# The first modulation of a diffusion layer: where three blocks sum their shift tiles, and which engine makes one affine

## The chip, the core and the metric

The kernel runs on one core of one Trainium2 chip. The time is the device time of one execution in microseconds; the time of a kernel is the median of its runs. One further execution is recorded by the profiler; its instructions, engines and waits are what "the profile" and "the trace" mean below. The engines are TensorE (PE in the profile; PEld are its weight loads), VectorE (DVE), ScalarE (ACT), GpSimd (POOL) and SyncE (SP), whose queue issues most of the DMA transfers.

## The reference

One layer of a diffusion backbone over 256 context tokens and 256 latent tokens of width 2048: a half-step SwiGLU feed-forward, token mixing, a second half-step feed-forward and a final norm. Ahead of each part stands an RMSNorm with a shift and a scale that come from a condition vector. What the change touches is the first of them, for both sequences:

```
def rms_norm(x, g):
    xf = x.astype(jnp.float32)
    y = xf * lax.rsqrt(jnp.mean(xf * xf, axis=-1, keepdims=True) + RMS_EPS)
    return (y * g.astype(jnp.float32)).astype(x.dtype)

def adaln(x, g, mod, i):
    return rms_norm(x, g) * (1 + mod[:, i + 1, None, :]) + mod[:, i, None, :]

def half_step_ffn(x, mod, i, g, w_up, w_down):
    h = adaln(x, g, mod, i)
    a, b = jnp.split(h @ w_up, 2, axis=-1)
    return x + 0.5 * mod[:, i + 2, None, :] * ((jax.nn.silu(a) * b) @ w_down)
...
        mod_l = (silu_c @ w_mod[l] + b_mod[l]).reshape(B, N_MOD, D_MODEL)
        mod_c = (silu_cc @ w_mod[l] + b_mod[l]).reshape(1, N_MOD, D_MODEL)
        xl = half_step_ffn(xl, mod_l, 0, g_norm[l, 0], w_ffn1_up[l], w_ffn1_down[l])
        xc = half_step_ffn(xc, mod_c, 0, g_norm[l, 0], w_ffn1_up[l], w_ffn1_down[l])
```

Everything is float32. The kernel keeps that precision by splitting an operand into a rounded part and the rest (`hi` and `lo`, `hhi` and `hlo`) and adding three products.

## The kernel before

**Tiles and blocks.** The width of 2048 is cut into 16 contraction tiles of 128 columns. In the beginning (lines 460 to 690) shift and scale of the first norm are computed tile by tile, together with the first products of the up projection: `BLOCKS` holds tiles 0 and 1 as blocks of one, then seven blocks of two (2 and 3, 4 and 5, up to 14 and 15). The code names a block by its bounds `k0`, `k1`.

**Shift and scale of a block.** Each is a product of a vector of 2048 (SiLU of the condition, one for each sequence) with 128 columns of `w_mod`. There are two ways.

On TensorE (`mod_sums`, line 563): a unit of weights (`mraw`, 128 x 2048, 1 MB) is multiplied with `cP`, the two condition vectors as 32 columns. The four strips of the array work on different contraction tiles, so a PSUM buffer holds four partial sums. ScalarE copies it to `row`; `mod_turned` (line 587) transposes the row on TensorE into another PSUM buffer, and VectorE reduces that to the column of `SH` (shift) or `SC` (scale) and adds the bias (`biased`).

On VectorE (lines 658 to 662): the unit lies transposed, and one SCALAR_TENSOR_TENSOR of 2048 columns for each sequence multiplies it with `cB`, the condition spread over all partitions, and sums along the row into `SH`.

In a block of two, VectorE sums the shift of the first tile and TensorE that of the second tile (`mod_sums(0, k1 - 1, k1)`, one unit of 16 multiplications, two records each) and the scales of both tiles (`mod_sums(1, k0, k1)`, two units of 8 wider ones). That is four units for a block. `mod_unit` loads them in the order of use into a ring of four `mraw` buffers (`bufs=4`, line 559), on SP's queue, which takes its loads in order.

**What follows in a block.** After the sums come `mod_turned`, `scale_of` (the scale times the gain of the norm), and `to_hT` (line 368), once for each sequence: TensorE transposes x into a PSUM buffer, and `affine_split` makes hhi, h and hlo from it. ScalarE makes both tiles of hhi and the first of h, VectorE the second of h (line 387) and hlo = h - hhi.

**Filler.** `products` (line 406) is a generator: the matmuls of a block with the weights of the first six halves of the up projection, in six steps of six matmuls for a block of two. The products of the block before (`prods`) are issued between the sums of this one, the last two steps after `to_hT` (`drain(prods)`). The weights of this block's products (`following`) are loaded between the units of scale and split on ScalarE (hi) and VectorE (lo) ahead of `mod_turned`.

**Order.** In this stage VectorE, TensorE and SP's loads keep the order of the program (`Pinned`, `keep_in_program_order`), ScalarE's order is left to the scheduler from the block of tile 2 on. `tbank` gives the PSUM buffers of this stage: a ring of two, for the sums, for the turned rows and for the transposed x alike. Each waits until the one two places before it was read.

Recorded operations have line 87 in the profile where a helper issues them, so tiles and not lines tell them apart.

Of the kernel before, what the change touches and what calls it, by code (L numbers as in the profile page):

```python
# [12 lines left out]
FP8 = mybir.dt.float8e5  # L13
AF = mybir.ActivationFunctionType
# [5 lines left out]
P = 128  # L20
# [20 lines left out]
PACE += (86, 102), (92, 109), (98, 118), (100, 130), (103, 144), (106, 152), (109, 163), (112, 170), (128, 181)  # L41

BLOCKS2 = tuple((k, k + 4) for k in range(0, 16, 4))

BLOCKS = ((0, 1), (1, 2)) + tuple((k, k + 2) for k in range(2, 16, 2))
FB = 4
# [12 lines left out]
def tile_layer(ctx: ExitStack, tc: tile.TileContext, I: dict, out: bass.AP):  # L59
# [319 lines left out]
    def affine_split(src, n, pairs, hh, hl):  # L379

        h = scratch[-1].tile([P, 2, 256], F32, tag="h", name="h", bufs=2)
        cols = [(SC[:, n, s, k : k + 1], SH[:, n, s, k : k + 1]) for k, s in pairs]
        if n != 1:
            for kk, (sc, sh) in enumerate(cols):
                scalar[0].activation(hh[:, kk, :], src[:, kk, :], AF.Identity, scale=sc, bias=sh)
        scalar[0].activation(h[:, 0, :], src[:, 0, :], AF.Identity, scale=cols[0][0], bias=cols[0][1])
        vector[0].tensor_scalar(h[:, 1, :], src[:, 1, :], *cols[1], op0=ALU.mult, op1=ALU.add)
        if n == 1:
            scalar[0].activation(hh, h, AF.Copy)
        vector[0].tensor_tensor(hl, h, hh.bitcast(F32), op=ALU.subtract)  # L390
# [70 lines left out]
    with pool(name="st", bufs=1) as st:  # L461
# [94 lines left out]
        def mod_unit():  # L556
            if ready:
                return ready.pop(0)
            raw = st.tile([P, 2048], F32, tag="mraw", name="mraw", bufs=4)
            tc.keep_in_program_order(nc.sync.dma_start(raw, I["w_m0"][next(unit)]))  # L560
            return raw

        def mod_sums(i, k0, k1, last=iter(())):

            n = (k1 - k0) * P
            nk = 2048 // n
            b = tbank()[:, :n]
            for g in range(KT // nk):
                if g == KT // nk - 1:
                    steps(last)  # L570
                raw = mod_unit()
                for j in range(nk):
                    k = nk * g + j
                    q = 32 * (j % 4)
                    tensor[0].matmul(
                        b[q : q + 32, :], cP[:, k, :], raw[:, j * n : (j + 1) * n], start=k < 4, stop=k >= KT - 4, tile_position=(0, q), skip_group_check=True
                    )
                yield
            row = st.tile([P, 256], F32, tag="row", name="row", bufs=3)[:, :n]
            scalar[0].activation(row, b, AF.Copy)  # L580
            turns.append((i, k0, k1, row))

        def biased(i, k0, k1):
            dst = (SH, SC)[i][:, 0, :, k0:k1]
            vector[0].tensor_tensor(dst, dst, bmT[:, i, k0:k1].unsqueeze(1).to_broadcast([P, 2, k1 - k0]), op=ALU.add)
# [61 lines left out]
        for k0, k1 in BLOCKS[1:]:  # L647
            kk = slice(k0, k1)
            following = products(1, pre, k0, k1, hhi, hlo, middle=True)
            if k1 - k0 == 2:  # L650
                raw = mod_unit()
            for i in range(2):
                for _ in mod_sums(i, k0 if i else k1 - 1, k1, following if i else iter(())):
                    steps(prods, 3 - (k1 - k0))
                if rest:
                    others(2, True)
                if not i and k1 - k0 == 2:
                    for s in (CTX, LAT):
                        vector[0].scalar_tensor_tensor(
                            junk.bitcast(FP8), raw, 1.0, cB[:, s, :], op0=ALU.mult, op1=ALU.mult, accum_out=SH[:, 0, s, k0 : k0 + 1], saturate=False  # L660
                        )
                    biased(0, k0, k0 + 1)

            if k0 != 2:
                steps(following)
            mod_turned()
            if k0 != 2:
                steps(prods)
            for s in (CTX, LAT):
                scale_of(0, s, kk)  # L670
            if k0 == 2:
                steps(following)
                steps(prods)
            if k1 - k0 == 1:
                tb = tbank()
                for s in (CTX, LAT):
                    for t in range(2):
                        x_turned(k0, s, t, tb)
                x_scaled(k0, tb)
            else:  # L680
                for s in (CTX, LAT):
                    drain(to_hT([xs0[s, 0], xs0[s, 1]], 0, s, hhi, hlo, 256 * s, range(k0, k1)))
            drain(prods)
            prods = following
            if k0 == 2:
                scalar[0] = nc.scalar
            if k1 == KT:
                nc.sync.dma_start(ccd.rearrange("s (k p) -> (s k) p", p=P), cc)
# [1659 lines left out]
def _laid_out(a):  # L2348
    asc = np.ascontiguousarray
    part = lambda v: v.reshape(-1, P).T  # L2350
    m = {
        "x": asc(a["x"][0]),
        "ctx": asc(a["ctx"][0]),
        "cc": asc(np.concatenate([a["c_ctx"].reshape(KT, P), a["c"].reshape(KT, P)])),
        "b_mod": asc(a["b_mod"][0].reshape(9, D)),
        "gate_b": asc(a["gate_b"][0]),
        "m_gain": asc(a["m_gain"][0]),
        "q_gain": asc(a["q_gain"][0]),
        "k_gain": asc(a["k_gain"][0]),
        "g_final": asc(a["g_final"]),  # L2360
        "rope": _rope_tables(),
    }
    cw = a["conv_w"][0].T.reshape(16, P, 5).transpose(1, 0, 2).reshape(P, 80)
    m["vecs"] = asc(np.concatenate([part(a["b_mod"][0]), part(a["g_norm"][0]), cw, part(a["conv_b"][0])], 1))

    wm = a["w_mod"][0].reshape(D, 9, D)

    def units(i, a_, b):
        n = (b - a_) * P
        k = 2048 // n  # L2370
        return wm[:, i, a_ * P : b * P].reshape(KT // k, k, P, n).transpose(0, 2, 1, 3).reshape(KT // k, P, 2048)

    def block(k0, k1):

        still = [wm[:, 0, k0 * P : (k0 + 1) * P].T[None]] if k1 - k0 == 2 else []
        return still + [units(0, k1 - 1, k1), units(1, k0, k1)]

    m["w_m0"] = asc(np.concatenate([u for b in BLOCKS for u in block(*b)]))
    m["w_mt"] = asc(wm[:, 2:].reshape(D, 7, KT, P).transpose(1, 2, 3, 0))
    for n in "12":  # L2380
        up, dn = a[f"w_ffn{n}_up"][0], a[f"w_ffn{n}_down"][0]
        nf = dn.shape[0] // P
        up = up.reshape(KT, P, 2, nf, P)

        rest = up[:, :, :, FB:].reshape(4, 4, P, 2, nf // FB - 1, CB)
        m[f"w_up{n}b"] = asc(rest.transpose(4, 3, 0, 2, 1, 5).reshape(nf // FB - 1, 2, 4, P, 2048))
        first = up[:, :, :, :FB].transpose(3, 2, 1, 0, 4).reshape(-1, 2, P, 2048)
        m[f"w_up{n}"] = asc(first[NPRE:])
        pre = first[:NPRE].reshape(2 * NPRE, P, KT, P)
        loads = []  # L2390
        for k0, k1 in BLOCKS if n == "1" else BLOCKS2:
            most = min(2 * NPRE, 2048 // ((k1 - k0) * P) // 2 * 2)
            loads += [pre[u : u + most, :, k0:k1].transpose(1, 0, 2, 3).ravel() for u in range(0, 2 * NPRE, most)]
        m[f"w_pre{n}"] = asc(np.concatenate(loads))
        m[f"w_dn{n}"] = asc(dn.reshape(NF // FB, FB, P, NCB, CB).transpose(0, 3, 2, 1, 4).reshape(NF // FB, NCB, P, 2048))
    w = a["w_in"][0]

    def tokens_still(cols):
        n = cols.shape[1]
        return asc(cols.reshape(4, 4, P, n).transpose(0, 2, 1, 3).reshape(4, P, 4 * n))  # L2400

    def tokens_move(c0):
        return asc(w[:, c0 : c0 + 1024].reshape(KT, P, NH, P).transpose(2, 1, 0, 3).reshape(NH, P, 2048))

    m["w_a"] = tokens_still(np.concatenate([w[:, GT0:], w[:, MV0 : MV0 + 384]], 1))
    m["w_b"] = tokens_still(w[:, MV0 + 384 : MV0 + 768])
    m["w_c"] = asc(w[:, MV0 + 768 : MV0 + 1024].reshape(2, 8, P, 256).transpose(0, 2, 1, 3).reshape(2, P, 2048))
    m["w_mk"], m["w_mq"] = tokens_move(MK0), tokens_move(MQ0)
    m["w_kv"] = tokens_still(w[:, AK0 : AK0 + 512])
    for c in range(2):  # L2410
        m[f"w_q{c}"] = tokens_still(w[:, AQ0 + 512 * c : AQ0 + 512 * (c + 1)])
        m[f"w_o{c}"] = tokens_still(w[:, MO0 + 512 * c : MO0 + 512 * (c + 1)])
    m["w_out"] = asc(a["w_out"][0].reshape(4, 4, P, NCB, CB).transpose(3, 0, 2, 1, 4).reshape(NCB, 4, P, 2048))
    return m
# [15 lines left out]
```

## Time and profile before

| | |
|---|---|
| time, median of 3 runs | 2605.07 us (2602.81 to 2609.3) |
| profiled execution, its time | 2604.58 us |
| its span in the trace | 2602.7 us |
| mean granted clock of TensorE | 0.996 |
| the beginning up to the last block's products | 0 to 126.5 us |

In the rows of the timeline the columns are start and length in us, engine, line, operation, the tiles written and read (`tr` and `mm` are PSUM buffers, `raw` the weights of products, `junkv` what the sums write beside their result), shapes, count, and in brackets the idle time before it with what ended it. A row with a count merges neighbours that run on. The chain of waits is the work that ended last, followed back; in its rows stand start, length, engine and tile. A matmul's length contains its latency, so the pace is read from starts.

### The profile page before, as it was taken

The page shows a single profiled execution, that of the slowest core. Times are in us where ns is not written, and L with a number is a line of the kernel's source. Part 1 is how long each engine was busy: PE and PEld are TensorE (multiplying, and loading weights), DVE is VectorE, ACT ScalarE, POOL GpSimd, SP SyncE. Part 2 cuts the span into 40 slices and gives each one's busy share as a digit, 9 for nine tenths or more (in the row PEclk, how much of TensorE's full clock was granted, in tenths as well). Part 3 has the DMA queues.
Part 4 walks back from the last instruction along what each step waited for, and adds up shares of the span by engine and source line. Part 5 has one row for each costly group of instructions (what it writes and reads, how often), then busy time and mean ns, then how long its engine had stood idle before and what let it go on. Part 6 is the DMA issues. An engine that isn't in the chain of part 4 may idle for free.

```text
span 2602.7 us, 33781 instructions
## 1 busy us (share of the span) xinstructions
PE 2575.7 (99%) x12670; PEld 2144.7 (82%) x12670; DVE 2170.6 (83%) x2864; ACT 1417.7 (54%) x1810; POOL 220.7 (8%) x269
## 2 busy tenths in 40 slices
PE   8999999999999999999999999999999999999998
PEld 5788888888888888888889889888897888888887
DVE  7788888878888788888887889798889878887887
ACT  4454444544444565444454347456476676666664
POOL 0000000100000100000110000120000000000001
PEclk8999999999999999999999999999999999999999
DMA  9889999999999988889987887776768988999876
GB/s 392 350 217 265 276 277 271 262 273 285 261 287 265 278 247 240 218 215 228 225 253 266 296 312 247 242 273 213 267 239 240 269 269 260 272 273 279 256 231 176
DMA packets 127219, 681.01 MB, mean 262 GB/s; under 512 B 14152, under 2 KB 16712, under 8 KB 64976
## 3 DMA queue, kind: packets, MB, share of 16 engines
q1 hardware_dynamic: 98544, 493.25, 50.7%
q0 software_dynamic: 28512, 185.61, 36.4%
q8 instruction: 99, 1.62, 0.2%
q14 instruction: 64, 0.52, 0.1%
HBM read 660.91 MB, written 17.89 MB: 261 GB/s over the span
## 4 chain that ended last, share of the span: by engine, by line
PE 85%; DVE 7%; DMA 5%; issue 2%; ACT 1%; POOL 0%; ACTq 0%; POOLq 0%; SPq 0%; DVEq 0%
PE mm L151 21%; PE mm L150 21%; PE mm L149 21%; DVE lo L128 2%; PE mm L87 2%; PE Y L149 2%; PE Y L151 2%; PE Y L150 2%; PE X L151 2%; PE X L150 2%; PE X L149 2%; PE tr L150 1%; PE tr L149 1%; PE tr L151 1%; PE tr L87 1%
## 5 line engine op out<-in xcount | busy, mean ns | idle before, releaser
L127 ACT ACTIVATE hi<-raw 128x1024 fp32r<-128x1024 f32 (+2 forms) x500 | 517.8, 1041 | 421.1 <-PE mm L151 264.1
L128 DVE TENSOR_TENSOR lo<-raw,hi 128x1024 fp32r<-128x1024 f32 (+2 forms) x488 | 583.6, 1207 | 149.7 <-ACT hi L127 130.5
L127 ACT ACTIVATE hi<-chain 128x1024 fp32r<-128x1024 f32 x336 | 355.0, 1059 | 305.7 <-PE mm L151 188.0
L128 DVE TENSOR_TENSOR lo<-chain,hi 128x1024 fp32r<-128x1024 f32 x336 | 407.2, 1221 | 118.0 <-ACT hi L127 114.3
L149 PE MATMUL mm<-hi,hhi 128*128 128x512 f32 (+3 forms) x1024 | 393.6, 385 | 0.0
L151 PE MATMUL mm<-hi,hlo 128*128 128x512 f32 (+3 forms) x1024 | 386.7, 378 | 0.0
L150 PE MATMUL mm<-lo,hhi 128*128 128x512 f32 (+3 forms) x1024 | 386.7, 378 | 0.0
L207 DVE SCALAR_TENSOR_TENSOR junk<-sraw,cBh 128x1024 fp8e5<-128x1024 f32 x192 | 234.3, 1220 | 19.2 <-DMA sraw<-in_w_mt 16.7
L151 PEld LDWEIGHTS mm<-hi,hlo 128*128 128x128 f32 x1024 | 192.5, 188 | 33.9
L149 PEld LDWEIGHTS mm<-hi,hhi 128*128 128x128 f32 x1024 | 192.6, 188 | 31.0
L150 PEld LDWEIGHTS mm<-lo,hhi 128*128 128x128 f32 x1024 | 192.8, 188 | 30.7
L128 DVE TENSOR_TENSOR lo<-ra,hi 128x1024 fp32r<-128x1024 f32 x96 | 117.0, 1223 | 39.7 <-ACT hi L127 35.8
L127 ACT ACTIVATE hi<-ra 128x1024 fp32r<-128x1024 f32 x96 | 101.9, 1061 | 65.1 <-PE mm L151 48.4
L149 PE MATMUL mm<-hi,hid2h 128*128 128x512 f32 x352 | 137.1, 390 | 0.0
L151 PE MATMUL mm<-hi,hid2l 128*128 128x512 f32 x352 | 137.0, 389 | 0.0
L150 PE MATMUL mm<-lo,hid2h 128*128 128x512 f32 x352 | 136.9, 389 | 0.0
L207 DVE SCALAR_TENSOR_TENSOR sr<-sr,cBl 128x1024 f32<-128x1024 f32 x84 | 103.0, 1234 | 14.7 <-DMA sr<-in_w_mt 13.8
L730 POOL DMA_DIRECT2D chain<-in_w_up1b x60 | 53.1, 886 | 726.0 <-DVE lo L128 648.9
L149 PE MATMUL mm<-hhi,hi 128*128 128x512 f32 (+1 forms) x288 | 101.4, 352 | 0.0
L151 PE MATMUL mm<-hhi,lo 128*128 128x512 f32 (+1 forms) x288 | 99.0, 344 | 0.0
L150 PE MATMUL mm<-hlo,hi 128*128 128x512 f32 (+1 forms) x288 | 98.7, 343 | 0.0
L149 PE MATMUL mm<-hi,sumshl 128*128 128x512 f32 x200 | 77.8, 389 | 0.0
(517 smaller groups left out, 5650.3 us busy)
## 6 DMA issues: line engine op xcount, KB each, us to landing
raw<-in_w_dn SPq DMA_DIRECT2D x70, 1024.0 KB, 7.5
chain<-in_w_up1b POOLq DMA_DIRECT2D x60, 1024.0 KB, 9.8
sraw<-in_w_mt SPq DMA_DIRECT2D x96, 512.0 KB, 7.8
sr<-in_w_mt SPq DMA_DIRECT2D x81, 512.0 KB, 5.5
raw<-in_w_up1b SPq DMA_DIRECT2D x40, 1024.0 KB, 7.9
mraw<-in_w_m SPq DMA_DIRECT2D x32, 1024.0 KB, 7.4
raw<-in_w_up2b SPq DMA_DIRECT2D x32, 1024.0 KB, 9.9
chain<-in_w_dn POOLq DMA_DIRECT2D x30, 1024.0 KB, 8.6
```

Of the source, the lines that this page charges most:

```text
L87: ins = getattr(self.engine, name)(*a, **k)
L127: scalar[0].activation(hi, src, AF.Copy)
L128: vector[0].tensor_tensor(lo, src, hi.bitcast(F32), op=ALU.subtract)
L149: tensor[0].matmul(out_ap, sh, mh, start=first, stop=False, skip_group_check=skip)
L150: tensor[0].matmul(out_ap, sh, ml, start=False, stop=False, skip_group_check=skip)
L151: tensor[0].matmul(out_ap, sl, mh, start=False, stop=last, skip_group_check=skip)
L207: ins = nc.vector.scalar_tensor_tensor(junk() if junk else raw, raw, 1.0, cB[s], op0=ALU.mult, op1=ALU.mult, accum_out=mT[:, i, s, kt, h : ...
L730: accum = lambda dst, src: nc.gpsimd.dma_start(dst, src, accum_op=ALU.add)
```

## The change

In the blocks that begin with tile 4, 8 or 12 (`BOTH`), VectorE sums the shift of both tiles: four SCALAR_TENSOR_TENSORs instead of two, each pair followed by the bias. TensorE's unit for the second tile's shift is gone there, and with it the row copied by ScalarE, its transpose and its reduction; one step of products that stood behind it stays. The other blocks of two sum as before. The host lays the second shift tile transposed into `w_m0` for these blocks; number, size and order of the loads stay.

In `affine_split`, where the number of the norm `n` is 0, ScalarE makes the second tile of h as well, for both sequences and all blocks of the beginning. For the later norms VectorE makes it as before.

```diff
+BOTH = (4, 8, 12)
...
         scalar[0].activation(h[:, 0, :], src[:, 0, :], AF.Identity, scale=cols[0][0], bias=cols[0][1])
-        vector[0].tensor_scalar(h[:, 1, :], src[:, 1, :], *cols[1], op0=ALU.mult, op1=ALU.add)
+        if n:
+            vector[0].tensor_scalar(h[:, 1, :], src[:, 1, :], *cols[1], op0=ALU.mult, op1=ALU.add)
+        else:
+            scalar[0].activation(h[:, 1, :], src[:, 1, :], AF.Identity, scale=cols[1][0], bias=cols[1][1])
...
             following = products(1, pre, k0, k1, hhi, hlo, middle=True)
-            if k1 - k0 == 2:
-                raw = mod_unit()
+            shifts = {k: mod_unit() for k in range(k0, k1 - (k0 not in BOTH))}
             for i in range(2):
-                for _ in mod_sums(i, k0 if i else k1 - 1, k1, following if i else iter(())):
+                for _ in mod_sums(i, k0 if i else k1 - 1, k1, following if i else iter(())) if i or k0 not in BOTH else "s":
                     steps(prods, 3 - (k1 - k0))
                 if rest:
                     others(2, True)
-                if not i and k1 - k0 == 2:
+                if i:
+                    continue
+                for k, raw in shifts.items():
                     for s in (CTX, LAT):
                         vector[0].scalar_tensor_tensor(
-                            junk.bitcast(FP8), raw, 1.0, cB[:, s, :], op0=ALU.mult, op1=ALU.mult, accum_out=SH[:, 0, s, k0 : k0 + 1], saturate=False
+                            junk.bitcast(FP8), raw, 1.0, cB[:, s, :], op0=ALU.mult, op1=ALU.mult, accum_out=SH[:, 0, s, k : k + 1], saturate=False
                         )
-                    biased(0, k0, k0 + 1)
+                    biased(0, k, k + 1)
...
-        still = [wm[:, 0, k0 * P : (k0 + 1) * P].T[None]] if k1 - k0 == 2 else []
-        return still + [units(0, k1 - 1, k1), units(1, k0, k1)]
+        still = [wm[:, 0, k * P : (k + 1) * P].T[None] for k in range(k0, k1 - (k0 not in BOTH))]
+        return still + ([] if k0 in BOTH else [units(0, k1 - 1, k1)]) + [units(1, k0, k1)]
```

## The prediction

> **What bounds the kernel now.** I read the busy shares first, then three stages by time, then one block of the beginning on each engine.
>
> ```profile
> span 2602.7 us, 33781 instructions
> PE 2575.7 (99%) x12670; PEld 2144.7 (82%) x12670; DVE 2170.6 (83%) x2864; ACT 1417.7 (54%) x1810; POOL 220.7 (8%) x269
> ```
>
> ```profile
> 30.00:126.50 96.50, 92.99 (x774) 64.80 (x772) 71.13 (x129) 38.79 (x75) 0.00 (x0) 0.98 0.94 374
> 126.50:2602.70 2476.20, 2459.03 (x11724) 2064.99 (x11724) 2076.40 (x2684) 1359.89 (x1696) 216.55 (x256) 1.00 0.87 256
> ```
>
> The windows list, after the length, the busy time of PE, its weight loads, VectorE (DVE), ScalarE (ACT) and GpSimd, then PE's granted clock, the DMA share and GB/s. The edit lies between 30 and 126.5 us; behind it PE is idle for 2476.20 - 2459.03 = 17.2 us in all, so a microsecond lost or won in the beginning reaches the end nearly whole. In the beginning VectorE and DMA are close behind PE. The block of tiles 8 and 9 (the second of the three edited ones) on PE, from the chain of waits (start, length, both us):
>
> ```profile
> 72.63 1.01 PE tr L87 x32
> 73.64 1.58 PE mm L87 x6
> 75.22 1.00 PE tr L87 x16
> 76.22 1.60 PE mm L87 x6
> 77.83 1.00 PE tr L87 x16
> 78.83 1.59 PE mm L87 x6
> 80.42 0.33 PE tr L87 x3
> 80.74 1.41 PE mm L87 x6
> 82.15 0.87 PE tr L87 x8
> 83.03 2.75 PE mm L87 x12
> 85.78 0.23 PE tr L87
> ```
>
> These are, in order, the shift of tile 9 (32 records, 1.01 us), the scale of both tiles in two units (16 each), three turned rows, eight transposes of x, and between them six units of products for the block before. PE has no gap: 85.78 - 72.63 = 13.15 us. The same block on VectorE, and ScalarE at its end:
>
> ```profile
> 72.95 0.69 DVE L87 TENSOR_TENSOR hlo<-h,hhi 128x512 fp32r<-128x512 f32 x1
> 73.56 2.29 DVE L87 SCALAR_TENSOR_TENSOR junkv<-mraw,cB 128x2048 fp8e5<-128x2048 f32 x1
> ...
> 75.88 2.29 DVE L87 SCALAR_TENSOR_TENSOR junkv<-mraw,cB 128x2048 fp8e5<-128x2048 f32 x1
> ...
> 78.30 1.83 DVE L87 TENSOR_TENSOR lo<-raw,hi 128x768 fp32r<-128x768 f32 x2
> 80.56 0.17 DVE L87 TENSOR_REDUCE SH<-tr 128x2 f32<-128x8 f32 x1 [0.44 <-PE tr L87]
> 80.77 0.17 DVE L87 TENSOR_TENSOR SH<-SH,vecs 128x2 f32<-128x2 f32 x1
> 80.84 0.17 DVE L87 TENSOR_REDUCE SC<-tr 128x4 f32<-128x16 f32 x1
> 81.05 0.16 DVE L87 TENSOR_TENSOR SC<-SC,vecs 128x4 f32<-128x4 f32 x1
> 81.24 0.23 DVE L87 SCALAR_TENSOR_TENSOR SC<-SC,vecs 128x2 f32<-128x2 f32 x2
> ```
>
> ```profile
> 82.63 1.02 ACT L385 ACTIVATE hhi<-tr,SH,SC 128x256 fp32r<-128x256 f32 x2 [3.29 <-PE tr L87]
> 83.54 0.56 ACT L386 ACTIVATE h<-tr,SH,SC 128x256 f32<-128x256 f32 x1
> 83.99 1.03 ACT L385 ACTIVATE hhi<-tr,SH,SC 128x256 fp32r<-128x256 f32 x2
> ```
>
> ```profile
> 84.14 0.54 DVE L87 TENSOR_SCALAR h<-tr,SC,SH 128x256 f32<-128x256 f32 x1 [2.67 <-ACT h L386]
> 84.72 0.69 DVE L87 TENSOR_TENSOR hlo<-h,hhi 128x512 fp32r<-128x512 f32 x1
> 85.51 0.54 DVE L87 TENSOR_SCALAR h<-tr,SC,SH 128x256 f32<-128x256 f32 x1
> ```
>
> The reader is to see how little room VectorE has before the reduction of the scale: the splitting ends at 78.30 + 1.83 = 80.13, and the reductions, which wait for PE, begin at 80.56. That is 0.43 us of room, whatever VectorE's average is.
>
> **The change part by part.** All is pinned in program order; VectorE's queue decides. I call h the moment at which VectorE ends the last hlo of the block before (here 72.95 + 0.69 = 73.64).
>
> *Removed from PE*, in each of three blocks: the 32 records of the shift unit, 1.01 us, and one of three row transposes, 0.33 / 3 = 0.11. That is 1.12 us a block and 3.4 us in all, if PE stays the bound.
>
> *Added to VectorE*: two more sums over 2048 columns. From the first sum to the splitting are 78.30 - 73.56 = 4.74 us for two sums with their accumulator reads, 78.30 - 73.64 = 4.66 after h; each pair costs 4.66 at that pace. The order of the built program puts both pairs ahead of the splitting, and the splitting ahead of the reduction of the scale. So the splitting ends at h + 2 x 4.66 + 1.83 = h + 11.15, and the reduction at h + 11.3, where before it ended 80.84 + 0.17 - 73.64 = 7.37 after h. The reduction of the shift that goes (80.84 - 80.56 = 0.28 with its bias) does not help; it came later in the queue.
>
> *Moved to ScalarE*: the line tests the number of the norm, 0 here, and not the sequence, so the second tile's affine of both sequences moves, in every block. ScalarE starts one every 0.45 us (83.54 to 83.99; the two hhi from 82.63 to 83.54 likewise). Eight in a row end at 82.63 + 8 x 0.45 + 0.11 = 86.34 (0.56 long, 0.45 apart: 0.11 of tail), then a hlo of 0.69: 87.05 and some 0.03 of handing over, 87.08. Before it was the last affine at 85.51 + 0.54 and a hlo of 0.69, 86.74. So the move makes hlo later by 0.33 us, though it takes 2 x 0.54 us off VectorE: h lies 87.08 - 85.78 = 1.3 us after the start of a block.
>
> *Which wait ends last.* The transposes of x go into the two PSUM buffers that the rows used before; those of the second sequence take the buffer that the reduction of the scale reads. In the shortened block PE needs it early: the first sequence's transposes end at half of 0.87 behind 82.15, 9.95 after the block's start, less 1.12, plus a wait at the start. There PE now begins with products instead of the shift, and the third pair of matmuls needs hlo at about 4/6 x 1.58 = 1.05, when it comes at 1.3: 0.3 us. So PE is there at 9.95 - 1.12 + 0.3 = 9.1 and the buffer is free at 1.3 + 11.3 = 12.6: PE stands 3.5 us. Queued behind are half of the transposes (0.43) and the last twelve products (2.75), which need nothing of VectorE. The block ends at h + 11.3 + 0.05 + 0.43 + 2.75 = h + 14.5, which is 15.8 after its start against 13.15: **2.7 us lost**, for the blocks from tiles 8 and 12.
>
> The block from tile 4 has a later h:
>
> ```profile
> 43.98 1.02 ACT L87 ACTIVATE hhi<-tr,SH,SC 128x256 fp32r<-128x256 f32 x2 [2.00 <-PE tr L87]
> ```
>
> ```profile
> 59.48 0.56 PE tr L87 x13
> ```
>
> Eight affines from 43.98, then hlo: h = 43.98 + 3.71 + 0.03 + 0.69 = 48.4, end 62.9 against 59.48: 3.4 us lost.
>
> The blocks between them have only 4.66 of sums. Their h is SC at h + 11.15 + 0.63 (80.84 to 81.47 for reduction, bias and scale), then eight affines and hlo, about h + 16.3, against a PE start at h + 14.5 and a first need 1.01 + 1.05 later, 16.6: no new wait, and no gain, since PE paces them. The stage's end waits for one late hlo more: 0.3. Sum of the waits: 3.4 + 2.7 + 2.7 + 0.3 = 9.1 us.
>
> *The clock behind a standing PE.* An earlier gap shows it (length, PE busy, instructions, granted clock, DMA share, GB/s):
>
> ```profile
> 36.70:38.90 2.20, 0.04 (x1) 1.00 1.01 425
> 38.90:40.40 1.50, 1.47 (x18) 0.90 1.01 415
> 40.40:43.40 3.00, 3.00 (x11) 0.50 1.01 429
> ```
>
> After 2.2 us without work the clock was 0.50 for 3.0 us: 1.5 us of work lost there, 0.15 before. A gap of 3.5 us should do as much, except where the slow time begins inside the gap. Bounds: 0 and 1.7 us a gap; I take 1.2, nearer to the row since the gap is longer, 3.6 us for three. The Trainium skill ("TensorE: Matmul & The Clock Gate", Part 1: The HAM clock gate) has the clock halved only after a whole idle window of about 3.4 us, on windows that run freely; by that a gap of 3.5 would hardly ever hold one, and the sum would be 9.1. The row, with 2.2 us of gap, speaks against it.
>
> *DMA.* The same 32 transfers run in the same order, but the slot of the second shift tile is freed by the fourth sum, at h + 9.3, instead of by PE at the block's start. Behind it wait, on SP's queue, two units, the products' weights and one unit more: 3.9 MB, 9.3 us at 420 GB/s (from 415 to 429 in the rows above), landing near h + 20.5. PE wants the last at h + 14.5 + 1.2 of clock + 5.2 (77.83 - 72.63) = h + 20.9. Nothing taken, bounds 0 and 2 us a block.
>
> Sum: 9.1 + 3.6 = 12.7 us, on the profiled execution's 2604.58 us (1.9 above its span, 0.5 below the median of the runs, 2605.07): **2617.3 us**.
>
> **The rivals.**
> VectorE keeps pace on average. Its work in a pair of blocks fits:
>
> ```profile
> 72.63:85.78 13.15, 13.15 (x116) 9.29 (x119) 9.71 (x18) 4.98 (x10) 0.00 (x0) 1.00 0.94 365
> ```
>
> That is 9.71 - 1.08 in the plain block and 9.71 - 1.08 + 4.66 in the other, 21.9 of some 25 us. If it could run ahead of PE, the change would win its 3.4 us: 2601.2, not slower. It decides by the moment at which the scale's reduction frees the PSUM buffer: at or before 9.1 after the block's start. Against it: 12.6 by the queue.
>
> The clock stays full in the gaps: 2604.58 + 9.1 = 2613.7. Against it stands the row at 40.4. For it stands the Trainium skill's rule above.
>
> Transfers late by their upper bound, 2 us in three blocks: 2623. For it the DMA share of 0.94; against it that PE's own delay gives them time.
>
> The delay is made up later, out of the 17.2 us that PE idles there: perhaps half of it, 2611. Against it: that is 0.7% of the stage, and its waits are not for transfers started early.
>
> That only one sequence's affine moves, as the summary may be read, would take 0.3 us from each block, 2616; the condition and the built order exclude it.
>
> **How the numbers follow.** The forecast 0.64, its own range 2613 to 2621 by the clock's bounds and 1 us of hand-over; full clock 0.14; late transfers 0.07; made up 0.09; VectorE keeping pace 0.06. The range 2609 to 2622 leaves out the last, half of the late transfers and half of what is made up, with some 0.03 unknown. The bound of 0.3% (what can be told from no change) lies at 2605.07 +/- 7.8. Slower, above 2612.9: 0.61 of the forecast, 0.12 of the full clock, 0.07 of the late transfers, 0.80. Faster, below 2597.3, is reached by no case's own number; half of keeping pace, 0.03, is left for it. Same is the rest, 0.03 + 0.02 + 0.09 + 0.03 = 0.17.
>
> **What would show it.** Right: in blocks 4, 8 and 12 four sums stand back to back ahead of the splitting, PE waits about 3.5 us at the transposes of x of the second sequence for VectorE's SC, the clock reads 0.5 near there, and the plain blocks keep 13.1 to 13.2 us. The first work behind the beginning (126.5 before) comes 11 to 14 us later. Wrong: no such gap, edited blocks of 12.0 us (PE still the bound), gaps that fall on transfers instead, or a delay at 126.5 that is gone at the end.

## The result, and the profile after

The changed kernel takes 2620.53 us (median of 6 runs, 2617.07 to 2624.63) against 2605.78 us before in the same comparison: 14.7 us more, a ratio of 1.0053 with a 95% interval of 1.0041 to 1.0065. The forecast was 2617.3 us, which is 12.7 us more than the 2604.58 us that it started from.

The windows of the changed kernel, with the border of the stages put behind the last products of the beginning (columns as in the prediction: length, busy time of PE, weight loads, VectorE, ScalarE, GpSimd, granted clock, DMA share, GB/s):

```profile
30.00:141.00 111.00, 95.45 (x675) 65.53 (x675) 76.32 (x124) 44.39 (x87) 0.00 (x0) 0.94 0.81 325
141.00:2617.40 2476.40, 2459.12 (x11724) 2064.65 (x11722) 2075.30 (x2683) 1359.51 (x1695) 214.00 (x256) 1.00 0.87 256
```

The long stage is unchanged: 2476.40 us with 2459.12 busy, where it was 2476.20 with 2459.03. Nearly all the loss lies in the beginning, where TensorE now stands 111.00 - 95.45 = 15.6 us (3.5 before), and where the mean granted clock fell from 0.98 to 0.94.

The first edited block (tiles 4 and 5) in the timeline of the changed kernel, rows of VectorE and TensorE alone:

```profile
48.03 2.28 DVE L89 SCALAR_TENSOR_TENSOR junkv<-mraw,cB 128x2048 fp8e5<-128x2048 f32 x1
...
55.10 2.29 DVE L89 SCALAR_TENSOR_TENSOR junkv<-mraw,cB 128x2048 fp8e5<-128x2048 f32 x1
55.54 0.60 PE L89 MATMUL tr<-ident,xs 128*128 128x128 f32 x4
57.51 1.83 DVE L89 TENSOR_TENSOR lo<-raw,hi 128x768 fp32r<-128x768 f32 x2
59.25 0.17 DVE L89 TENSOR_REDUCE SC<-tr 128x4 f32<-128x16 f32 x1
59.48 0.66 PE L89 MATMUL tr<-ident,xs 128*128 128x128 f32 x4 [3.33 <-DVE SC L89]
64.41 1.08 PE L89 MATMUL tr<-mraw,cP 128*32 128x128 f32 x32
```

The four sums run from 48.03 without a pause, the splitting follows at 57.51 and the reduction of the scale at 59.25. TensorE has transposed x of the first sequence at 55.54 and then stands 3.33 us, until that reduction has read the PSUM buffer. The eight affines and the products come behind it. The other two edited blocks repeat it, here on TensorE, with the work behind each gap; the last row is the last products of the beginning:

```profile
90.32 0.66 PE L89 MATMUL tr<-ident,xs 128*128 128x128 f32 x4 [3.36 <-DVE SC L89]
95.25 1.08 PE L89 MATMUL tr<-mraw,cP 128*32 128x128 f32 x32
...
121.15 0.66 PE L89 MATMUL tr<-ident,xs 128*128 128x128 f32 x4 [3.37 <-DVE SC L89]
126.08 1.08 PE L89 MATMUL tr<-mraw,cP 128*32 128x128 f32 x32
...
140.67 0.73 PE L89 MATMUL mm<-hlo,hi 128*128 128x512 f32 x2 [0.46 <-DVE hlo L89]
```

What TensorE waited for between 30 and 150 us (total, times, longest):

```profile
PE tr L89 <- DVE SC L89: 10.1, 3, 3.4
PE mm L89 <- DVE hlo L89: 2.5, 5, 0.9
PE tr L89 <- DMA mraw<-in_w_m: 2.2, 1, 2.2
```

Three waits for the scale make 10.1 us. The one wait for a transfer, 2.2 us long, ends at 38.6 us, ahead of the edited blocks; the kernel before has it too (it ends at 38.9).

A row with 32 records of mraw is the shift unit with which a plain block begins; its start is a good mark, since one edited and one plain block lie between two of them. The same marks before:

```profile
59.41 1.08 PE L87 MATMUL tr<-mraw,cP 128*32 128x128 f32 x32
...
85.71 1.08 PE L87 MATMUL tr<-mraw,cP 128*32 128x128 f32 x32
...
112.00 1.08 PE L87 MATMUL tr<-mraw,cP 128*32 128x128 f32 x32
117.51 1.07 PE L87 MATMUL tr<-mraw,cP 128*32 128x256 f32 x16 [0.24 <-DMA mraw<-in_w_m]
126.57 0.73 PE L87 MATMUL mm<-hlo,hi 128*128 128x512 f32 x2 [0.17 <-DVE hlo L87]
```

A pair of blocks took 26.30 us (59.41 to 85.71) and takes 30.84 (64.41 to 95.25). The delay is 5.0 us at the first mark, 9.5 at the second, 14.1 at the third and 14.1 at the last products (126.57 to 140.67). Part of it is the clock, in the windows of the changed kernel (length, PE busy, instructions, clock, DMA share, GB/s):

```profile
55.90:59.50 3.60, 0.27 (x4) 1.00 1.01 426
60.30:63.50 3.20, 3.20 (x9) 0.50 1.04 436
```

Behind the gap the clock reads 0.50 for 3.2 us. From the transposes at 59.48 to the next block's start at 64.41 are 4.93 us, and the same 4.93 behind the other two gaps.

### The profile page after: what moved, and what is told of

It reads as the page before. It is cut to its first block, busy times and chain, and to the rows that moved or that the text cites. A ratio compares the mean times of both kernels' runs of the same rounds, so it can differ in the third digit from the quotient of the medians.

```text
span 2617.4 us, 33562 instructions
## 1 busy us (share of the span) xinstructions
PE 2578.1 (99%) x12571; PEld 2145.1 (82%) x12571; DVE 2174.8 (83%) x2858; ACT 1422.9 (54%) x1822; POOL 218.2 (8%) x269
```

## The experiments

Theory Q is the prediction's: VectorE's queue holds the PSUM buffer that the transposes need. Theory K is its second half: the gap halves the clock for a time. Each ratio below is against the kernel before. The start of the first edited block differs by up to two microseconds from execution to execution, so pairs of marks are compared in the traces, and not single moments.

### The affine alone

```diff
-BOTH = (4, 8, 12)
+BOTH = ()
```

> Only the affine moves to ScalarE; no block sums both shift tiles on VectorE. Theory Q (the scale's reduction stands behind four sums and the splitting in VectorE's queue and holds the PSUM buffer that TensorE's transposes need): hlo comes 0.3 us later in a block, behind TensorE's shift unit, so the time is that of before within 1 us (2605 to 2607) and the last products of the beginning start at 126.6 to 127.2 us. Rival A (ScalarE's longer chain of affines causes the loss): 3 to 5 us slower than before, about a third of the 14.7.

2606.5 us, ratio 1.0002 (0.9993 to 1.0012). In its trace on TensorE:

```profile
58.48 1.08 PE L89 MATMUL tr<-mraw,cP 128*32 128x128 f32 x32
...
84.78 1.08 PE L89 MATMUL tr<-mraw,cP 128*32 128x128 f32 x32
91.44 1.07 PE L89 MATMUL tr<-mraw,cP 128*32 128x256 f32 x16 [1.40 <-DMA mraw<-in_w_m]
```

The first pair takes 26.30 us, to the hundredth what it took before. The one difference up to the third mark is a wait of 1.40 us for a transfer in the second pair. Rival A falls: ScalarE's longer chain is hidden behind the shift unit.

### The sums alone

```diff
-        if n:
-            vector[0].tensor_scalar(h[:, 1, :], src[:, 1, :], *cols[1], op0=ALU.mult, op1=ALU.add)
-        else:
-            scalar[0].activation(h[:, 1, :], src[:, 1, :], AF.Identity, scale=cols[1][0], bias=cols[1][1])
+        vector[0].tensor_scalar(h[:, 1, :], src[:, 1, :], *cols[1], op0=ALU.mult, op1=ALU.add)
```

> The three blocks sum both shift tiles on VectorE; the affine stays divided as before. Theory Q: nearly all of the loss stays, 0.3 us less a block: 2618 to 2620.5 us, three gaps of TensorE of 3.2 to 3.5 us at the transposes of the second sequence, last products of the beginning at 139 to 140.7 us. Rival A: less than half of the loss, under 2613 us.

2617.48 us, ratio 1.0047 (1.0035 to 1.0060): 0.5 us under the range of Q, far above that of A. Three gaps of 3.33 to 3.35 us stand at the same place.

```profile
63.92 1.08 PE L89 MATMUL tr<-mraw,cP 128*32 128x128 f32 x32
89.50 0.66 PE L89 MATMUL tr<-ident,xs 128*128 128x128 f32 x4 [3.33 <-DVE SC L89]
94.42 1.08 PE L89 MATMUL tr<-mraw,cP 128*32 128x128 f32 x32
```

A pair takes 30.50 us, 0.34 less than in the change. So the affine costs 0.34 us a block where nothing covers it, which is in the edited blocks, since these begin without the shift unit.

### The splitting behind the scale's reduction

```diff
-            if k0 != 2:
+            late = k0 == 2 or k0 in BOTH
+            if not late:
                 steps(following)
             mod_turned()
-            if k0 != 2:
+            if not late:
                 steps(prods)
...
-            if k0 == 2:
+            if late:
                 steps(following)
                 steps(prods)
```

> The change, with the splitting of the products' weights moved behind the scale's reduction in the three blocks. Theory Q: the PSUM buffer comes free 1.83 us earlier, the gap falls from 3.35 to 1.5 us in each block; 5.5 us are won if the clock still halves (2615 us) and up to 10.7 if a gap of 1.5 us leaves it full (2610 us). Rival D (transfers freed late by the second pair of sums set the gap): the sums end when they did, so no change, 2620 us.

2608.86 us, ratio 1.0015 (1.0006 to 1.0024), 1 us better than the better of Q's two numbers.

```profile
84.38 0.66 PE L89 MATMUL tr<-ident,xs 128*128 128x128 f32 x4 [1.63 <-DVE SC L89]
87.72 1.08 PE L89 MATMUL tr<-mraw,cP 128*32 128x128 f32 x32
```

The gap falls from 3.36 to 1.63 us, by 1.73 where the splitting is 1.83 long, and the transposes and products behind it take 87.72 - 84.38 = 3.34 us instead of 4.93: the clock stayed full behind the shorter gap. A pair takes 27.51 us (60.21 to 87.72). The sums end when they did in the change, and the gap moved with the reduction alone, which rival D did not allow.

### The gap filled with matmuls that add zeros

```diff
                     drain(to_hT([xs0[s, 0], xs0[s, 1]], 0, s, hhi, hlo, 256 * s, range(k0, k1)))
+                    for _ in range(14 if s == CTX and k0 in BOTH else 0):
+                        tensor[0].matmul(pre[0][0], zr, hhi[:, 0, :], start=False, stop=False, skip_group_check=True)
```

> The change, with 14 matmuls of a zero tile added into one of the accumulating PSUM banks, between the transposes of the first and of the second sequence in the three blocks; they add zeros and take about 14 x 0.23 = 3.2 us where TensorE stands 3.35 us. Theory K (the gap halves the clock afterwards, and that costs 1.75 us a block): the granted clock stays 1.00, the wait for VectorE stays as long in sum, and 5.2 us are won: 2615.3 us, last products of the beginning at 135.5 us. Rival C (the slow time after the gap is not the gap's doing): no change, 2620 us, or a loss.

2612.65 us, ratio 1.0025 (1.0016 to 1.0035), 2.6 us better than K's number.

```profile
59.00:62.00 3.00, 3.00 (x31) 1.00 1.03 434
```

```profile
83.77 3.45 PE L89 MATMUL mm<-hhi,zr 128*128 128x512 f32 x14
87.34 0.66 PE L89 MATMUL tr<-ident,xs 128*128 128x128 f32 x4
90.70 1.08 PE L89 MATMUL tr<-mraw,cP 128*32 128x128 f32 x32
```

The added matmuls end where VectorE's reduction does, the granted clock stays 1.00, and the work behind takes 90.70 - 87.34 = 3.36 us. A pair takes 29.27 us (61.43 to 90.70), 1.57 less than in the change though TensorE has more to do. At the last products of the beginning the two traces are 6.1 us apart (140.67 and 134.55). Of these, 4.7 lie behind the three gaps, and 1.4 ahead of them, where the change had a clock of 0.50 from 39.81 to 43.22 us and this execution had not. The rest of the 7.9 us between the two medians was not traced to a cause.

### The remaining products ahead of the second sequence

```diff
                     drain(to_hT([xs0[s, 0], xs0[s, 1]], 0, s, hhi, hlo, 256 * s, range(k0, k1)))
+                    if k0 in BOTH:
+                        drain(prods)
```

> The change, with the last twelve products of the block before (2.75 us) moved ahead of the second sequence's transposes in the three blocks, so that work that needs nothing of VectorE stands in the gap. Theory Q with K: the gap at the transposes falls from 3.35 to 0.6 us and the clock stays full there, 4.5 us a block; but VectorE's chain (four sums, splitting, scale, affines, hlo) is no shorter, and TensorE meets it 2.4 us later at the first hlo of the next block. Two blocks then take 28.2 to 28.4 us (30.84 in the change, 26.30 before), up to 30 if that second gap halves the clock: 2612 to 2617 us. Rival (only the order on TensorE costs): all of 4.5 us a block comes back, 26.3 us for two blocks, 2607 us.

2614.33 us, ratio 1.0034 (1.0021 to 1.0046), in the middle of Q's range.

```profile
61.84 1.08 PE L89 MATMUL tr<-mraw,cP 128*32 128x128 f32 x32 [1.77 <-ACT h L392]
64.40 0.73 PE L89 MATMUL mm<-hlo,hi 128*128 128x512 f32 x2 [0.35 <-DVE hlo L89]
...
88.35 0.66 PE L89 MATMUL tr<-ident,xs 128*128 128x128 f32 x4 [0.60 <-DVE SC L89]
90.77 1.73 PE L89 MATMUL tr<-mraw,cP 128*32 128x128 f32 x32 [1.76 <-ACT h L392]
```

The gap at the transposes is 0.60 us, and 2.1 us of waiting come back in the next block (1.77 and 0.35), where 2.4 was expected at hlo alone. Most of it stands earlier than expected: the shift unit needs the PSUM buffer that the first sequence's affines still read. The first pair takes 28.93 us, within Q's numbers between full and half clock. Behind the second block's waits the clock was 0.50 from 91.05 to 94.46 us; behind the other two it stayed full. Better order on TensorE alone does not mend it; the chain on VectorE and ScalarE is too long for an edited block.

### Both moves, and the same in all blocks

`both_moves` has the last two diffs together. `late_skip` has the late splitting in every block of two, and in the plain blocks behind edited ones no step of products between the shift unit and the first unit of scale; `late_skip_v` divides the affine as before.

```diff
                 for _ in mod_sums(...) if i or k0 not in BOTH else "s":
+                    if not i and k0 - 2 in BOTH:
+                        continue
                     steps(prods, 3 - (k1 - k0))
...
+            late = k0 >= 2
```

> Both moves at once in the three blocks: the splitting behind the scale's reduction, and the twelve products ahead of the second sequence's transposes. Theory Q: the reduction ends 9.5 us after the last hlo, before TensorE comes to it, so no gap at the transposes; hlo is ready 14.5 after the last one, 1.4 us after TensorE needs it in the next block. Two blocks take 26.6 us, 0.3 more than before: 2606 to 2608 us. Rival D (late transfers): gaps on the weight units appear and hold two blocks above 27.5 us, 2610 us.

> As both_moves, with the splitting behind the scale's reduction in all blocks of two, and in the blocks that follow the three the first step of products moved behind the first unit of scale, which gives hlo 1.0 us more. Theory Q: the wait at hlo falls from 1.4 to 0.4 us, two blocks take 25.6 us against 26.30 before, 1.5 to 2.5 us faster than before in all (2603 to 2604.5 us). Rival D: transfers bound two blocks at 26.3 us or more (9.96 MB at 380 GB/s), no gain, 2605.5 us or slower.

> As late_skip, with the affine divided between ScalarE and VectorE as before. Theory Q: the wait of 0.3 to 0.5 us at the first hlo of the three blocks goes, since hlo comes 0.33 us sooner there; behind the three blocks hlo comes at the same time or 0.3 us later, since VectorE's affine queues behind the splitting. Two blocks take 25.2 to 25.7 us: 2602.5 to 2604.5 us. Rival D as for late_skip: 26.3 us or more.

Each was expected to be faster than it is. They take 2610.97 us (ratio 1.0014, 1.0005 to 1.0022), 2609.61 us (1.0016, 1.0007 to 1.0025) and 2609.14 us (1.0012, 1.0004 to 1.0021). The first has no wait left at the transposes and none for transfers in its pairs, so its miss is not rival D's; its pair takes 27.20 us, 0.6 more than Q's sum:

```profile
60.41 1.08 PE L89 MATMUL tr<-mraw,cP 128*32 128x128 f32 x32 [0.83 <-ACT h L392]
...
87.61 1.08 PE L89 MATMUL tr<-mraw,cP 128*32 128x128 f32 x32 [0.82 <-ACT h L392]
```

The last, whose waits on TensorE between 30 and 142 us are led by transfers, has pairs of 26.61 and 26.10 us:

```profile
PE tr L89 <- DMA mraw<-in_w_m: 7.2, 6, 1.7
```

```profile
58.47 1.08 PE L89 MATMUL tr<-mraw,cP 128*32 128x128 f32 x32 [0.19 <-DVE h L89]
...
85.08 1.08 PE L89 MATMUL tr<-mraw,cP 128*32 128x128 f32 x32
...
111.18 1.08 PE L89 MATMUL tr<-mraw,cP 128*32 128x128 f32 x32
```

Here rival D holds in part. The 26.10 us of the second pair are 0.2 under the kernel before, and at the third mark this execution is 0.8 us ahead of it (111.18 against 112.00). Of the 7.2 us of waits for weight units that have not landed, 2.5 lie ahead of the first mark; behind it are 4.7, where the kernel before has 0.24, and 3.0 of them stand in the last plain block:

```profile
113.87 1.07 PE L89 MATMUL tr<-mraw,cP 128*32 128x256 f32 x16 [1.61 <-DMA mraw<-in_w_m]
117.93 1.07 PE L89 MATMUL tr<-mraw,cP 128*32 128x256 f32 x16 [1.41 <-DMA mraw<-in_w_m]
```

The first work behind the beginning (line 152, 150 before) then starts 1.3 us later than before (135.52 against 134.19). The other 4.9 us by which this execution's span is longer lie behind that point. From there to the end the fourteen traces differ by up to 5.4 us (2468.0 to 2473.4), so what these orders cost there is not shown. No version beat the kernel before. A fifth mraw buffer, which might let the loads start sooner, was not tried.

### One edited block, and the clock once more

```diff
-BOTH = (4, 8, 12)
+BOTH = (8,)
```

> The change with both shift tiles summed by VectorE in one block only, that of tiles 8 and 9. Theory Q with K: one gap of 3.35 us and one time at half clock behind it, 4.5 us more than before for the two blocks from 59 to 86 us on (30.84 for 26.30), the other blocks 26.30 a pair; 2610 to 2611 us. Rival (a price paid once, as the beginning leaves its balance with the transfers, and not for each block): 2615 us or more.

2609.74 us, ratio 1.0018 (1.0009 to 1.0027).

```profile
58.22 1.08 PE L89 MATMUL tr<-mraw,cP 128*32 128x128 f32 x32
72.82 0.73 PE L89 MATMUL mm<-hlo,hi 128*128 128x512 f32 x2 [0.48 <-DVE hlo L89]
84.13 0.66 PE L89 MATMUL tr<-ident,xs 128*128 128x128 f32 x4 [3.37 <-DVE SC L89]
87.46 1.08 PE L89 MATMUL tr<-mraw,cP 128*32 128x128 f32 x32
```

```profile
84.10:87.50 3.40, 3.37 (x20) 1.00 1.03 434
```

The gap is as long as in the change, 3.37 us, but the clock behind it reads 1.00 and the work takes 3.33 us. The pair takes 29.24 us: 2.94 more than before, and 1.60 less than in the change. The median is 4.2 us above the kernel before, not the 14.7 of three blocks, so the price is not paid once but for each block. That a gap of this length always halves the clock was wrong, so the last three runs repeat the two kernels.

> The changed kernel once more, to see how often its gaps halve the clock. Theory K as held so far (a gap of 3.35 us always halves it): three gaps, three times at 0.50, 30.84 us for two blocks, as in the first trace. Theory R (the clock is judged on windows that run freely, and the gap halves it only where it covers enough of one): some gap is followed by full clock, and two blocks take 29.1 to 29.3 us there, as in the kernel with one edited block.

> As change_again_1, one execution more. Theory K: 30.84 us for both pairs of blocks. Theory R: at least one pair, here or in the other execution, at 29.1 to 29.3 us.

> The kernel with one edited block once more. Theory R: the gap of 3.35 us is followed by half clock in some executions and by full clock in others: 30.84 or 29.24 us for the two blocks. Rival (something in this kernel keeps the clock full behind its gap): 29.24 us again.

Single executions, of 2620.16, 2618.24 and 2609.1 us (the kernel before took 2608.66 beside them). In both further executions of the change all three gaps were followed by half clock, with pairs of 30.84 and 30.87 us for the first; in the second of one edited block the clock was full again (58.45 to 87.68, 29.23 us). So neither theory's expectation fits, and only the rival's number for the kernel with one edited block came out: with three edited blocks the clock fell behind nine gaps out of nine (and behind three of three in the kernel with the sums alone), with one edited block behind none of two. The last section shows what sets the two apart.

## Why the prediction was right

**The place of the wait: right.** Four sums, then the splitting, then the reduction, and TensorE standing at the second sequence's transposes. The gap was given as 3.5 us and is 3.33 to 3.37. Moving the reduction by moving the splitting moved the gap by nearly as much (1.73 of 1.83 us), and taking the sums away took it away.

**The price of the waits: nearly right.** For the blocks from tiles 8 and 12 the prediction had 2.7 us each; one edited block with full clock costs 29.24 - 26.30 = 2.94. Of the difference, 0.15 is the tail behind the gap, 3.33 us where 0.43 + 2.75 was summed, and 0.1 the hlo ahead of the sums, which ended 1.4 us after the block's start (72.76 against 58.22 + 13.15) and not 1.3. From there the queue took what was summed: the reduction began 11.14 us later (11.15). For the block from tile 4 it had 3.4; the first mark moved by 5.00, and without the 1.60 of clock that leaves 3.40. That this agrees to the hundredth is luck: the profiled execution of the change was already 0.36 us ahead of the one before at the wait for a transfer (38.58 and 38.94).

**The clock: right in kind, too small in size.** It was put at 1.2 us a gap between bounds of 0 and 1.7. Three gaps cost 3 x 1.60 = 4.8 us instead of 3.6 (4.93 with half clock, 3.33 without, for the same work). This is the term that was mis-sized, and 1.2 of the 2.0 us between the 12.7 us forecast and the 14.7 measured. (The 3.2 us between 2617.3 and 2620.53 hold 1.2 us more, by which the kernel before stood above 2604.58 in the same comparison.) That the slow time might begin inside the gap, the reason for taking less than the row, did not come true: in the three traces of the change it began 0.02 to 0.81 us behind the gap's end and lasted 3.41 us. Whether it comes at all hangs on how the gap lies in time, which the prediction did not work out; one edited block did not pay it. In so far, that all three blocks paid was luck.

**The sum.** 3.4 + 2 x 2.94 + 4.8 = 14.1 us, the delay at the last products. The terms come from the same marks and from the kernel with one block, so this shows where the time went and is no second measurement. The 0.3 us added for the end of the stage did not appear: TensorE waits 0.46 us for the last hlo instead of 0.17, but the wait for a transfer at 117.51 is gone. Between that point and the end of the span the change has 0.6 us more.

**The affine: right.** It costs 0.34 us where uncovered (0.33 was given, though 86.34 + 0.69 is 87.03 and not 87.05) and nothing alone, and it moved for both sequences.

**The rivals.** VectorE keeping pace on average did not come true, although its busy share would allow it: with one queue in order, 3.36 us of standing come of the place of the reduction, and not of the load. Late transfers do not set any of the three gaps, but bind in part when the gaps are closed (4.7 us behind the first mark in `late_skip_v`), and none of the orders here won the 3.4 us. The prediction's landing time for them, h + 20.5, is 1.9 us later than its own terms add up to (9.3 + 9.3 behind h); no run shows where the 1.9 comes from, and nothing hung on it, since the term was put at nothing, as it came out. Nothing was made up later. Full clock behind the gap was real in the kernel with one block.

## What to carry to other kernels

Work handed to an engine with spare time is paid for at the point in its queue where it stands, so look for what is released behind it, here the PSUM buffer that a small reduction reads. Moving that reduction ahead of work that nothing waits for won most of the loss back; evening out the load of the engines did not. A gap on TensorE can cost half as much again through the clock, so an estimate of a new gap should carry that term, with both ends of its range.

## What was not expected of the hardware

A gap of the same length and place acted on the clock in two ways. In the three traces with three edited blocks and in that with the sums alone, eleven gaps of 3.33 to 3.37 us and one of 2.81 were followed by 0.50; both gaps with one edited block, 3.37 and 3.33 us, by 1.00; and 2.2 us of standing in the kernel before by 0.50. So the length of a gap does not decide by itself. The Trainium skill ("TensorE: Matmul & The Clock Gate", Part 1: The HAM clock gate) says that activity is judged over windows of about 3.4 us which run freely; a gap would then count by how it lies over them, which would allow both outcomes. The traces agree: every stretch of one clock that ends before the last products of the beginning lasts 3.41, 10.24, 13.65, 17.07, 27.31, 30.72 or 47.79 us, which are whole multiples of 3.41. Let the time be cut into pieces of 3.41 us, counted from a moment at which the clock changes. The third gap of the kernel with the sums alone (first view) and the gap of the kernel with one edited block (second view) then look like this (length, PE busy, instructions, clock, DMA share, GB/s):

```profile
118.03:121.44 3.41, 1.45 (x9) 1.00 1.00 420
121.44:124.85 3.41, 3.41 (x9) 0.50 1.03 420
```

```profile
78.80:82.21 3.41, 1.96 (x12) 1.00 0.96 387
82.22:85.63 3.41, 1.50 (x9) 1.00 1.00 421
```

A border falls into the gap in both. In the first kernel the piece behind it holds 3.41 - 1.45 = 1.96 us without work, and half clock follows for the length of one piece. In the second the two pieces hold 1.45 and 1.91 us, and the clock stays full. With the pieces laid out like this in all fourteen traces, every one between 33 and 140 us that held 1.96 us or more of standing was followed by half clock (19 of them), and none that held 1.91 or less was. So a whole idle window, the condition that the prediction took from the Trainium skill, was not needed here, and the measurement decides: more than half of a piece was enough. The filled gaps and those of the late splitting fit this, since no piece held more than 1.63 us of standing there, and so do the 2.2 us in the kernel before, which lay in one piece. A pair of 30.84 us is nine pieces and 0.1 us, so the three gaps of one execution of the change lie almost alike and are not three independent cases. Whether other executions of these kernels fall the other way is not shown: three of the change were traced and two with one edited block.
